# Another order of products and direct sub-tiles in the first column pairs of the retention output projection

## The chip, the cores and the metric

The kernel runs on one core of a Trainium2 chip. The metric is the device time of one launch in microseconds (us). A core has a matrix engine (TensorE, "PE" in the profile, with its weight loads as "PEld"), a vector engine (VectorE, "DVE"), a scalar engine (ScalarE, "ACT"), GpSimd ("POOL") and SyncE ("SP"), which here only starts DMA transfers. Each works through its own instruction list in order; they wait for one another by semaphores. Matrix products land in PSUM banks, of which each holds 128 x 512 fp32 numbers.

## The reference

A decoder trunk of two layers on one sequence of 256 tokens and width 2048: layer 0 is gated linear attention (GLA, four heads), layer 1 is retention (eight heads). Each layer widens to 4096, has a SiLU gate and a residual, and a last RMS norm follows.

```
h = x
h = h + gla_mixer(rms_norm(h, gla_norm[0]), ...)        # layer 0
h = h + retention_mixer(rms_norm(h, ret_norm[0]), ...)  # layer 1
return rms_norm(h, final_norm)

def retention_mixer(h, positions, w_in, gn_g, gn_b, w_out):
    q, k, v, gate = split(h @ w_in)         # widths 2048, 2048, 4096, 4096
    ... rotary q/k, chunked retention, group norm -> o   # 256 x 4096
    return (o * silu(gate)) @ w_out         # 4096 -> 2048
```

The change concerns only this last product, `@ w_out` of the retention layer: 256 tokens, 4096 inputs, 2048 outputs, all fp32.

## The kernel before, in words

**Weights and products.** All weights are streamed from HBM as sub-tiles of 256 input rows by 512 columns (512 KB), through eight raw buffers (`NRAW`, L29). SP starts the load of a raw buffer as soon as the buffer's last reader is done (`emit_raws`, L249; L243). For an fp32 product on PE each sub-tile is split in two parts: `hi`, a rounded copy by ACT (L287), and `lo`, the rest, a subtraction on DVE (L288), into pairs of split tiles of which there are four. Splits are made `LOOK` = 3 sub-tiles ahead of their use (`emit_split` L273, `next_weights` L315). The activations are split in the same way beforehand, and each product is made of three matmuls, hi x hi, hi x lo and lo x hi (`three`, L392 to L397). A sub-tile that is used for 128 tokens and two input slices, or one with all 256 tokens, comes to 6 or 12 matmuls of 512 columns.

**The output product in halves.** The 4096 inputs are the eight heads' outputs; the output product is done in two halves, after four heads each (`out_half`). The first half's output tiles are named `ra`, the second half's `rb`; each has four groups of 512 columns. Groups 0 and 1 are always done as a pair (`out_pair`, L959, tiles `rae` and `rbe`). `ra` has a second pair, groups 2 and 3; in `rb` group 2 (`rb2`, banks `rb_ps`) is a plain group and group 3 is the tail (`out_tail`, L1078), in matmuls of 256 columns (`tail_ps`), with the final norm behind it.

**A pair.** A pair takes two neighbouring groups, the one called v (group c) and the one called g (group c+1). The products of their first four sub-tiles are done by a Strassen-like scheme: seven block products instead of eight, on sums of weights and on sums of activations (`rsum`). The tokens P1, P2, P3, P5, P6, P7 and P8 are these products; each needs two split sub-tiles and 12 matmuls. The other four sub-tiles of each group are used directly for all 256 tokens: tokens v4 to v7 and g4 to g7, one split sub-tile and 12 matmuls each. The order of the tokens is a string: `UNIT` for most pairs, `LATE` for the first pair of each retention half (`out_order`, L147). The token `z` only marks where the two v sub-tiles for the sums are loaded.

**Sums of raw weights.** P1 uses x (the first two g sub-tiles), P3 uses z (v's third and fourth). Both are then changed in place in their raw buffers: accumulating DMAs that POOL starts (L296) add further sub-tiles from HBM to them, and two DVE adds (L282) make x += z ahead of P6. P5 uses x after the first two v sub-tiles were added to it, P7 uses z after `z += v` (v's first two), P8 uses x after `x += g` (g's third and fourth). In `_plan` (`pair`, L72) each sub-tile carries, in `post`, the accumulating DMAs that are to be started behind its split.

**Banks.** A pair has four banks, `B, A, C, V1`, and one of a pool of two (`lev`) for P5. P1, P6, P7 go through A one after the other, each taken out before the next begins; P8 stays in A and the g sub-tiles of the second 128 tokens are added to it there, up to g7. P2 begins B, in which the g sub-tiles of the first 128 tokens follow. P3 begins C; C and V1 take the v sub-tiles.

**Joins.** What a bank holds is joined to the residual `resid` in SBUF by one DVE instruction of 128 x 512: an add (L993) or a subtraction (L995). For P7, ACT copies the bank out first (`u3`, L1025). Joins are put off by one token in the program (`pend`).

**Who sets the order.** The token strings set the order of the program text. A planner then orders the instructions of each engine anew by its own estimate of times, under what depends on what, so that side work (the last head's norm and gating, transposes `rot_tp`, tiles `ro`, `ogt`) is laid between the tokens, and single matmuls of a neighbouring sub-tile can be drawn ahead. Each engine's list is fixed from then on.

Of the kernel before, what the change touches and what calls it, by code (L numbers as in the profile page):

```python
# [10 lines left out]
F32 = mybir.dt.float32  # L11
# [6 lines left out]
P = 128  # L18
# [4 lines left out]
GW = 512  # L23
SUB = 2
NSUB = NKT // SUB
# [30 lines left out]
def _plan():  # L56


    loads, subs = [], []

    def load(gid, j):
        loads.append((gid, j))
        return len(loads) - 1

    def use(c, pre=None, post=()):
        subs.append((c, pre, post))

    def plain(gid, js=range(NSUB)):
        for j in js:
            use(load(gid, j))  # L70

    def pair(g, v, q=None, order=None):  # L72
        order = (order or UNIT).split()
        x = [load(g, 0), load(g, 1)] if order[0] == "P1" else []
        z = []
        later = max(("P3", "P6"), key=order.index)
        for n, tok in enumerate(order):
            kind, i = tok[0], tok[1:]
            if kind in "qvg":
                plain({"q": q, "v": v, "g": g}[kind], [int(i)])  # L80
            elif tok == "z":
                z += [load(v, 2), load(v, 3)]
            elif tok == "P2":
                plain(g, [2, 3])
            else:
                if tok == "P1" and not x:
                    x += [load(g, 0), load(g, 1)]
                for j in range(2):
                    post = []
                    if tok == later:  # L90
                        post.append((z[j], (v, j)))
                    if tok == "P1":
                        post.append((x[j], (v, j)))
                    if tok == "P6":
                        post.append((x[j], (g, 2 + j)))
                    use(z[j] if tok in ("P3", "P7") else x[j], z[j] if tok == "P6" else None, post)

    def out_cols_of(name, half, joint):
        for c in (0, 2):
            cols = [(name, half, c + n) for n in range(2)]  # L100
            if joint[c // 2]:
                pair(cols[1], cols[0], order=out_order(name, c))
                continue
            for x in cols:
                plain(x)

    for half in range(2):
        for h in (2 * half, 2 * half + 1):
            plain(("aqk", h))
            for g in (2 * h, 2 * h + 1):  # L110
                if g in JOINT["a"]:
                    pair(("ag", g), ("av", g))
                else:
                    plain(("av", g))
                    plain(("ag", g))
        out_cols_of("ao", half, JOINT["ao", half])
    for half in range(2):
        for h in range(4 * half, 4 * half + 4):
            pair(("rg", h), ("rv", h), ("rqk", h), ret_order(h))
# [12 lines left out]
    for c in range(len(loads)):  # L132
        b = min(range(NRAW), key=lambda n: free[n])
        buf.append(b)
        free[b] = last[c]
    return loads, subs, places, last, buf
# [4 lines left out]
WHOLE = " ".join(f"q{j}" for j in range(NSUB)) + " " + UNIT  # L141


LATE = "P1 v4 z P3 v5 P5 P6 P2 v6 P7 g4 g5 v7 P8 g6 g7"


def out_order(name, c):  # L147
    return LATE if (name, c) == ("ro", 0) else UNIT

# [16 lines left out]
def kernel(  # L166
# [33 lines left out]
    lev_p = pool("lev", 2, space=psum)  # L200
# [200 lines left out]
    def product(ps, left, stop=False):  # L401
        for j in range(2):
            hi, lo = next_weights()
            for q in range(SUB):
                k = j * SUB + q
                three(ps, left(k, 0), left(k, 1), hi, lo, q, stop and k == QK - 1)

    def direct(lhs, ps, j, stop=False):
        hi, lo = next_weights()
        for t in range(2):  # L410
            cols = slice(t * P, (t + 1) * P)
            for q in range(SUB):
                kt = j * SUB + q
                three(ps[t], lhs[:, kt, 0, cols], lhs[:, kt, 1, cols], hi, lo, q, stop and q == SUB - 1)
# [544 lines left out]
    def out_pair(c, first, final, name):  # L959
        lhs, s = ogt, cur["s"]  # L960
        B, A, C, V1 = acc(4, f"{name}e{c}_ps", which=list(slots))
        slots.rotate(-2)
        P5 = lev_p.tile([P, GW], F32, tag="lev", name=f"{name}e{c}_p5")
        plain = lambda kt0, t: lambda k, a: lhs[:, kt0 + k, a, t * P : (t + 1) * P]
        summed = lambda i: lambda k, a: s[i][:, k, a, :]
        u3 = t4_p.tile([P, 2, GW], F32, tag="t4", name=f"{name}e{c}_u3")[:, 0, :]

        if final:
            for col in (c, c + 1):
                norm_row(col)  # L970

        def whole(col, t):
            if not first:
                square_sum(t, col)
            if final:
                dst = cur["resid"][:, t, col * GW : (col + 1) * GW]
                nc.vector.tensor_tensor(dst, dst, fns[col], ALU.mult)

        onward = not (first or final)
        late = deque([out_transposes(c)] if onward else [])  # L980

        def turn():
            advance()
            if late:
                next(late[0], None)

        g = c + 1
        tt_done, pend = set(), []

        def join(col, t, src, op=ALU.add, mark=None):  # L990
            dst = cur["resid"][:, t, col * GW : (col + 1) * GW]
            if op == ALU.add:
                keep(nc.vector.tensor_tensor(dst, src, dst, ALU.add))  # L993
            else:
                keep(nc.vector.tensor_tensor(dst, dst, src, ALU.subtract))  # L995
            tt_done.add((col, t, mark))
            if all((col, t, m) in tt_done for m in parts[col - c][t]):
                whole(col, t)

        parts = ((("5", "6", "v"), ("5", "7", "v")), (("1", "g"), ("g",)))  # L1000
        products = {
            "P1": lambda: product(A, plain(0, 0), stop=True),
            "P2": lambda: product(B, plain(4, 0)),
            "P3": lambda: product(C, summed(0)),
            "P5": lambda: product(P5, summed(1), stop=True),
            "P6": lambda: product(A, summed(2), stop=True),
            "P7": lambda: product(A, summed(3), stop=True),
            "P8": lambda: product(A, plain(4, 1)),
        }
        joins = {  # L1010
            "P1": lambda: join(g, 0, A, mark="1"),
            "P5": lambda: [join(c, t, P5, mark="5") for t in range(2)],
            "P6": lambda: join(c, 0, A, ALU.subtract, "6"),
            "P7": lambda: join(c, 1, u3, ALU.subtract, "7"),
            "v7": lambda: [join(c, t, x, mark="v") for t, x in enumerate((C, V1))],
        }
        toks = [x for x in out_order(name[0] + "o", c).split() if x != "z"]
        for n, tok in enumerate(toks):
            if tok[0] == "P":
                products[tok]()  # L1020
            else:
                direct(lhs, (C, V1) if tok[0] == "v" else (B, A), int(tok[1:]), stop=tok[1:] == str(NSUB - 1))
            if tok == "P7":
                with tc.high_priority():
                    keep(nc.scalar.activation(u3, A, AF.Copy))  # L1025
            while pend:
                pend.pop(0)()
            if tok in joins:
                pend.append(joins[tok])
            if n < 4:  # L1030
                advance()
                step()
                if n == 3:
                    drain_side()
            elif tok in ("g5", "P8", "g6"):
                turn()
        join(g, 0, B, mark="g")
        join(g, 1, A, mark="g")
        if onward:
            for _ in late[0]:  # L1040
                pass
            tasks.append(out_transposes(g))
        begun.clear()
        closed.clear()
# [212 lines left out]
    def ret_head(h):  # L1257
# [276 lines left out]
```

## Time and profile before

| what | us |
|---|---|
| median of three runs | 1383.75 (1382.77 to 1383.86) |
| the profiled execution's own time | 1382.14 |
| its span in the profile | 1380.3 |
| PE busy | 1363.0 (99%) |
| DVE busy | 1105.1 (80%) |
| ACT busy | 850.0 (62%) |
| POOL busy | 142.2 (10%) |
| weight loads started by SP | 447, median 5.0 to landing |
| accumulating and other weight DMAs started by POOL | 96, median 7.2 to landing |

Times inside the profile count from the start of the span. The first pair of the first half (`rae`) lies at about 924 to 968 us, that of the second half (`rbe`) at about 1280 to 1327, the plain group and the tail at 1327 to 1380. A row of a timeline gives start, duration, engine, line, operation, output and inputs, and in brackets how long the engine had stood idle before it and who released it. A row of waits gives engine, what waited, whom it waited for, the sum in us, how often, and the longest. A PE row's duration is that of one matmul, of which the next begins before it ends; the time between two starts is what counts.

### The profile page before, as it was taken

The numbers are of one execution on the slowest core, as the hardware profiler recorded it, in microseconds if no ns is written. First come the engines' busy times: TensorE is split into PE (matmuls) and PEld (weight loads), VectorE is DVE, ScalarE is ACT, GpSimd is POOL, SyncE is SP. The second block draws the span as 40 slices with busy tenths as digits, with TensorE's granted clock in tenths as the row PEclk, the third lists the DMA queues.
The fourth block names the chain that finished last, engine by engine and source line by source line (L and its number), as shares of the span: only waits on it lengthen the run. The fifth ranks groups of instructions, "written<-read, shape, count | busy, mean of one in ns | idle before, by whom it ended". The sixth has DMA issues, their size and how long they took to land.

```text
span 1380.3 us, 18486 instructions
## 1 busy us (share of the span) xinstructions
PE 1363.0 (99%) x6608; PEld 1142.2 (83%) x6608; DVE 1105.1 (80%) x1533; ACT 850.0 (62%) x1122; POOL 142.2 (10%) x200
## 2 busy tenths in 40 slices
PE   9999999999999999999999999999999999999997
PEld 7888888888888888888888888887888888888787
DVE  6686795987778887769888898988868897888883
ACT  6576656655567747566666665665546666666562
POOL 1003020110021021001011010101100101011100
PEclk9999999999999999999999999999999999999999
DMA  9755555789658657868898887898898787889771
GB/s 365 249 175 166 175 168 183 170 243 346 195 157 266 193 177 197 305 168 248 283 304 204 253 206 242 212 305 248 214 365 233 218 276 190 248 215 314 186 269 62
DMA packets 85085, 317.15 MB, mean 230 GB/s; under 512 B 9840, under 2 KB 10864, under 8 KB 83712
## 3 DMA queue, kind: packets, MB, share of 16 engines
q1 hardware_dynamic: 66768, 240.55, 49.5%
q0 software_dynamic: 16784, 68.03, 24.9%
q10 hardware_dynamic: 1440, 7.38, 1.4%
q8 instruction: 52, 0.85, 0.2%
q14 instruction: 41, 0.34, 0.1%
HBM read 305.44 MB, written 10.49 MB: 229 GB/s over the span
## 4 chain that ended last, share of the span: by engine, by line
PE 93%; DVE 3%; DMA 2%; issue 1%; ACT 1%; POOL 0%; DVEq 0%; SPq 0%; ACTq 0%
PE rqk_ps L368 8%; PE re_ps L395 8%; PE re_ps L396 8%; PE re_ps L397 8%; PE rqk_ps L369 4%; PE gqk_ps L368 4%; PE gg_ps L326 3%; PE gv_ps L325 3%; PE gv_ps L326 3%; PE gv_ps L327 3%; PE gg_ps L327 3%; PE gg_ps L325 3%; DMA raw<-in_w_all 2%; PE ge_ps L396 2%; PE ge_ps L397 2%; PE ge_ps L395 2%
## 5 line engine op out<-in xcount | busy, mean ns | idle before, releaser
L288 DVE TENSOR_TENSOR lo<-raw,hi 128x1024 fp32r<-128x1024 f32 (+1 forms) x569 | 687.2, 1220 | 199.9 <-ACT hi L287 193.4
L287 ACT ACTIVATE hi<-raw 128x1024 fp32r<-128x1024 f32 (+1 forms) x569 | 596.1, 1056 | 385.3 <-DMA raw<-in_w_all 57.3
L368 PE MATMUL rqk_ps<-xhl,hi 128*128 128x512 f32 x480 | 161.7, 396 | 0.0
L296 POOL DMA_DIRECT2D raw<-in_w_all x96 | 83.0, 869 | 542.7 <-DVE lo L288 257.7
L396 PE MATMUL re_ps<-lo,xhl 128*128 128x512 f32 x352 | 137.3, 390 | 0.0
L397 PE MATMUL re_ps<-hi,xhl 128*128 128x512 f32 x352 | 137.1, 390 | 0.0
L395 PE MATMUL re_ps<-hi,xhl 128*128 128x512 f32 x352 | 131.7, 391 | 0.0
L369 PE MATMUL rqk_ps<-xhl,lo 128*128 128x256 f32 x480 | 121.4, 281 | 0.0
L368 PEld LDWEIGHTS rqk_ps<-xhl,hi 128*128 128x128 f32 x480 | 89.3, 188 | 17.5
L369 PEld LDWEIGHTS rqk_ps<-xhl,lo 128*128 128x128 f32 x480 | 87.5, 189 | 3.7
L397 PEld LDWEIGHTS re_ps<-hi,xhl 128*128 128x128 f32 x352 | 66.1, 188 | 13.7
L396 PEld LDWEIGHTS re_ps<-lo,xhl 128*128 128x128 f32 x352 | 66.1, 188 | 13.2
L395 PEld LDWEIGHTS re_ps<-hi,xhl 128*128 128x128 f32 x352 | 66.0, 188 | 13.3
L368 PE MATMUL gqk_ps<-xhl,hi 128*128 128x512 f32 x216 | 76.5, 398 | 0.0
L326 PE MATMUL gg_ps<-lo,xhl 128*128 128x512 f32 x192 | 75.4, 393 | 0.0
L326 PE MATMUL gv_ps<-lo,xhl 128*128 128x512 f32 x192 | 75.2, 392 | 0.0
L325 PE MATMUL gv_ps<-hi,xhl 128*128 128x512 f32 x192 | 75.1, 393 | 0.0
L327 PE MATMUL gv_ps<-hi,xhl 128*128 128x512 f32 x192 | 75.0, 391 | 0.0
L327 PE MATMUL gg_ps<-hi,xhl 128*128 128x512 f32 x192 | 74.9, 390 | 0.0
L325 PE MATMUL gg_ps<-hi,xhl 128*128 128x512 f32 x192 | 74.8, 391 | 0.0
L810 POOL TENSOR_TENSOR s<-s,m 128x64 f32<-128x64 f32 x56 | 36.1, 676 | 233.2 <-DVE m L801 223.9
L369 PE MATMUL gqk_ps<-xhl,lo 128*128 128x256 f32 x216 | 59.0, 280 | 0.0
(422 smaller groups left out, 2686.1 us busy)
## 6 DMA issues: line engine op xcount, KB each, us to landing
raw<-in_w_all SPq DMA_DIRECT2D x447, 512.0 KB, 5.0
raw<-in_w_all POOLq DMA_DIRECT2D x96, 512.0 KB, 7.2
resid<-in_x_n SPq DMA_DIRECT2D x2, 1024.0 KB, 8.6
gg<-in_gn_g POOLq DMA_DIRECT2D x8, 256.0 KB, 4.0
resid_x<-resid ACTq DMA_DIRECT2D x1, 2048.0 KB, 9.0
gb<-in_gn_b POOLq DMA_DIRECT2D x8, 256.0 KB, 7.4
gb_resid<-resid_x POOLq DMA_DIRECT2D x1, 2048.0 KB, 11.9
resid_g<-gb_resid ACTq DMA_DIRECT2D x1, 2048.0 KB, 9.9
```

The lines of the kernel that those rows point to most:

```text
L287: a = nc.scalar.activation(hi[:, sl], src[:, sl], AF.Copy)
L288: b = nc.vector.tensor_tensor(lo[:, sl], src[:, sl], hi[:, sl].bitcast(F32), ALU.subtract)
L296: nc.gpsimd.dma_start(raws[n], block(key), accum_op=ALU.add)
L325: mm(ps, xh, hi[:, q, :], start=kt == 0, stop=False)
L326: mm(ps, xh, lo[:, q, :], start=False, stop=False)
L327: mm(ps, xl, hi[:, q, :], start=False, stop=kt == NKT - 1)
L368: mm(ps[c], wh, rhs[:, kt, :, :], start=kt == 0, stop=False)
L369: mm(ps[c][:, 0, :], wl, rhs[:, kt, 0, :], start=False, stop=False)
L395: mm(ps, xh, hi[:, q, :], start=start, stop=False, **again)
L396: mm(ps, xh, lo[:, q, :], start=False, stop=False, **again)
L397: mm(ps, xl, hi[:, q, :], start=False, stop=stop, **again)
L810: nc.gpsimd.tensor_tensor(dst, dst, side_of(m[:, li, :], z), ALU.add)
```

## The change

Three things change, all for the first pair (columns 0 and 1) of each retention half.

The string `LATE` becomes another order. Before: `P1 v4 z P3 v5 P5 P6 P2 v6 P7 g4 g5 v7 P8 g6 g7`. After: `P1 v4 z P3 g4 P5 v5 P6 P2 g5 P7 v6 P8 g6 v7 g7`: direct sub-tiles and products take turns, g4 and g5 come before P7, and v7 is last but one.

Since g4 now comes before P6 and P7 need bank A, the g sub-tiles of the second 128 tokens get a bank of their own, `G1`, the second one of the pool `lev`. P8 then ends in bank A and is joined on its own (mark `8`), and the join of `G1` follows g7: one more join per pair.

In the plan, the accumulating DMAs `x += g` are no longer started behind P6's own two sub-tiles' splits in the `post` list of those, but are kept in `owed` and go with the next direct sub-tile or with P2's first: those of `z += v` come first. This part of the code holds for all pairs.

```
--- before.py
+++ after.py
@@ -74,14 +74,18 @@
         x = [load(g, 0), load(g, 1)] if order[0] == "P1" else []
         z = []
         later = max(("P3", "P6"), key=order.index)
+        owed = []
         for n, tok in enumerate(order):
             kind, i = tok[0], tok[1:]
             if kind in "qvg":
-                plain({"q": q, "v": v, "g": g}[kind], [int(i)])
+                use(load({"q": q, "v": v, "g": g}[kind], int(i)), post=owed)
+                owed = []
             elif tok == "z":
                 z += [load(v, 2), load(v, 3)]
             elif tok == "P2":
-                plain(g, [2, 3])
+                use(load(g, 2), post=owed)
+                plain(g, [3])
+                owed = []
             else:
                 if tok == "P1" and not x:
                     x += [load(g, 0), load(g, 1)]
@@ -92,7 +96,7 @@
                     if tok == "P1":
                         post.append((x[j], (v, j)))
                     if tok == "P6":
-                        post.append((x[j], (g, 2 + j)))
+                        owed.append((x[j], (g, 2 + j)))
                     use(z[j] if tok in ("P3", "P7") else x[j], z[j] if tok == "P6" else None, post)
 
     def out_cols_of(name, half, joint):
@@ -141,7 +145,7 @@
 WHOLE = " ".join(f"q{j}" for j in range(NSUB)) + " " + UNIT
 
 
-LATE = "P1 v4 z P3 v5 P5 P6 P2 v6 P7 g4 g5 v7 P8 g6 g7"
+LATE = "P1 v4 z P3 g4 P5 v5 P6 P2 g5 P7 v6 P8 g6 v7 g7"
 
 
 def out_order(name, c):
@@ -961,6 +965,10 @@
         B, A, C, V1 = acc(4, f"{name}e{c}_ps", which=list(slots))
         slots.rotate(-2)
         P5 = lev_p.tile([P, GW], F32, tag="lev", name=f"{name}e{c}_p5")
+        order = out_order(name[0] + "o", c)
+        G1 = A
+        if order == LATE:
+            G1 = lev_p.tile([P, GW], F32, tag="lev", name=f"{name}e{c}_g1")
         plain = lambda kt0, t: lambda k, a: lhs[:, kt0 + k, a, t * P : (t + 1) * P]
         summed = lambda i: lambda k, a: s[i][:, k, a, :]
         u3 = t4_p.tile([P, 2, GW], F32, tag="t4", name=f"{name}e{c}_u3")[:, 0, :]
@@ -997,7 +1005,7 @@
             if all((col, t, m) in tt_done for m in parts[col - c][t]):
                 whole(col, t)
 
-        parts = ((("5", "6", "v"), ("5", "7", "v")), (("1", "g"), ("g",)))
+        parts = ((("5", "6", "v"), ("5", "7", "v")), (("1", "g"), ("g", "8") if G1 is not A else ("g",)))
         products = {
             "P1": lambda: product(A, plain(0, 0), stop=True),
             "P2": lambda: product(B, plain(4, 0)),
@@ -1005,7 +1013,7 @@
             "P5": lambda: product(P5, summed(1), stop=True),
             "P6": lambda: product(A, summed(2), stop=True),
             "P7": lambda: product(A, summed(3), stop=True),
-            "P8": lambda: product(A, plain(4, 1)),
+            "P8": lambda: product(A, plain(4, 1), stop=G1 is not A),
         }
         joins = {
             "P1": lambda: join(g, 0, A, mark="1"),
@@ -1014,12 +1022,14 @@
             "P7": lambda: join(c, 1, u3, ALU.subtract, "7"),
             "v7": lambda: [join(c, t, x, mark="v") for t, x in enumerate((C, V1))],
         }
-        toks = [x for x in out_order(name[0] + "o", c).split() if x != "z"]
+        if G1 is not A:
+            joins["P8"] = lambda: join(g, 1, A, mark="8")
+        toks = [x for x in order.split() if x != "z"]
         for n, tok in enumerate(toks):
             if tok[0] == "P":
                 products[tok]()
             else:
-                direct(lhs, (C, V1) if tok[0] == "v" else (B, A), int(tok[1:]), stop=tok[1:] == str(NSUB - 1))
+                direct(lhs, (C, V1) if tok[0] == "v" else (B, G1), int(tok[1:]), stop=tok[1:] == str(NSUB - 1))
             if tok == "P7":
                 with tc.high_priority():
                     keep(nc.scalar.activation(u3, A, AF.Copy))
@@ -1035,7 +1045,7 @@
             elif tok in ("g5", "P8", "g6"):
                 turn()
         join(g, 0, B, mark="g")
-        join(g, 1, A, mark="g")
+        join(g, 1, G1, mark="g")
         if onward:
             for _ in late[0]:
                 pass
```

More of the change, by code (lines that the diff above doesn't have):

```diff
@@ L76, in pair @@
         later = max(("P3", "P6"), key=order.index)
+        owed = []
         for n, tok in enumerate(order):
@@ L79, in pair @@
             if kind in "qvg":
-                plain({"q": q, "v": v, "g": g}[kind], [int(i)])
+                use(load({"q": q, "v": v, "g": g}[kind], int(i)), post=owed)
+                owed = []
             elif tok == "z":
@@ L83, in pair @@
             elif tok == "P2":
-                plain(g, [2, 3])
+                use(load(g, 2), post=owed)
+                plain(g, [3])
+                owed = []
             else:
@@ L94, in pair @@
                     if tok == "P6":
-                        post.append((x[j], (g, 2 + j)))
+                        owed.append((x[j], (g, 2 + j)))
                     use(z[j] if tok in ("P3", "P7") else x[j], z[j] if tok == "P6" else None, post)
@@ L141 @@
 WHOLE = " ".join(f"q{j}" for j in range(NSUB)) + " " + UNIT
-LATE = "P1 v4 z P3 v5 P5 P6 P2 v6 P7 g4 g5 v7 P8 g6 g7"
+LATE = "P1 v4 z P3 g4 P5 v5 P6 P2 g5 P7 v6 P8 g6 v7 g7"
 def out_order(name, c):
@@ L963, in out_pair @@
         P5 = lev_p.tile([P, GW], F32, tag="lev", name=f"{name}e{c}_p5")
+        order = out_order(name[0] + "o", c)
+        G1 = A
+        if order == LATE:
+            G1 = lev_p.tile([P, GW], F32, tag="lev", name=f"{name}e{c}_g1")
         plain = lambda kt0, t: lambda k, a: lhs[:, kt0 + k, a, t * P : (t + 1) * P]
@@ L998, in join @@
                 whole(col, t)
-        parts = ((("5", "6", "v"), ("5", "7", "v")), (("1", "g"), ("g",)))
+        parts = ((("5", "6", "v"), ("5", "7", "v")), (("1", "g"), ("g", "8") if G1 is not A else ("g",)))
         products = {
@@ L1007, in out_pair @@
             "P7": lambda: product(A, summed(3), stop=True),
-            "P8": lambda: product(A, plain(4, 1)),
+            "P8": lambda: product(A, plain(4, 1), stop=G1 is not A),
         }
@@ L1016, in out_pair @@
         }
-        toks = [x for x in out_order(name[0] + "o", c).split() if x != "z"]
+        if G1 is not A:
+            joins["P8"] = lambda: join(g, 1, A, mark="8")
+        toks = [x for x in order.split() if x != "z"]
         for n, tok in enumerate(toks):
@@ L1021, in out_pair @@
             else:
-                direct(lhs, (C, V1) if tok[0] == "v" else (B, A), int(tok[1:]), stop=tok[1:] == str(NSUB - 1))
+                direct(lhs, (C, V1) if tok[0] == "v" else (B, G1), int(tok[1:]), stop=tok[1:] == str(NSUB - 1))
             if tok == "P7":
@@ L1037, in out_pair @@
         join(g, 0, B, mark="g")
-        join(g, 1, A, mark="g")
+        join(g, 1, G1, mark="g")
         if onward:
```

## The prediction

> **What bounds the kernel now.** I read the page first (busy shares, the chain that ended last), then PE's waits over the whole run, then the busy time of each engine in the stretches that the change touches, then single instructions.
>
> ```profile
> span 1380.3 us, 18486 instructions
> PE 1363.0 (99%) x6608; PEld 1142.2 (83%) x6608; DVE 1105.1 (80%) x1533; ACT 850.0 (62%) x1122; POOL 142.2 (10%) x200
> PE 93%; DVE 3%; DMA 2%; issue 1%; ACT 1%; POOL 0%; DVEq 0%; SPq 0%; ACTq 0%
> ```
>
> PE is busy 99% of the span and holds 93% of the chain. The change removes no matmul, so it can win only PE's waits, and adds time only by making new ones. All of PE's longest waits are these (us in total, times, longest):
>
> ```profile
> PE warm_ps L514 <- POOL warm L512: 1.8, 1, 1.8
> PE gqk_ps L356 <- ACT hi L287: 1.3, 1, 1.3
> PE rae_ps L395 <- DVE resid L995: 1.3, 1, 1.3
> PE rbe_ps L395 <- DVE resid L995: 1.3, 1, 1.3
> PE rbe_ps L395 <- ACT hi L287: 1.2, 1, 1.2
> PE rae_ps L395 <- ACT hi L287: 1.2, 1, 1.2
> ```
>
> Four of the six lie in the two pairs that the change rewrites (`rae`, `rbe`): 1.2 at P6 on the weight split, 1.3 at the first matmul of P7, which waits until L995 has taken P6 out of bank A. The next view (us; busy time of PE, PEld, DVE, ACT and POOL; PE clock; DMA share; GB/s) takes both pairs from P3 to that wait, and what follows:
>
> ```profile
> 929.50:951.90 22.40, 19.68 (x86) 14.85 (x84) 22.40 (x30) 11.86 (x13) 4.03 (x5) 1.00 0.65 148
> 951.90:966.30 14.40, 14.36 (x63) 11.91 (x64) 10.00 (x9) 8.23 (x9) 0.00 (x0) 1.00 1.00 377
> 1285.30:1307.70 22.40, 19.68 (x86) 14.83 (x84) 22.40 (x30) 11.85 (x13) 4.05 (x5) 1.00 0.64 146
> 1307.80:1327.10 19.30, 19.18 (x84) 15.55 (x85) 14.48 (x15) 10.71 (x13) 0.00 (x0) 1.00 0.98 356
> ```
>
> Here the whole-run average misleads: from P3 to the L995 join DVE is busy 22.40 of 22.40 us, PE only 19.68. In this stretch DVE is the bound; it is so because the split of each sub-tile (`lo`, one DVE instruction), the raw sums and the head's last side work meet. A product (P token) asks two splits for 12 matmuls, a direct sub-tile (v or g token) one split for 12. So what counts is how many matmuls PE has issued when DVE reaches the join that frees bank A.
>
> **The change part by part.** First the order.
>
> ```profile
> 951.95 0.50 PE L395 MATMUL rae_ps<-hi,rsum 128*128 128x512 f32 x1 [1.26 <-DVE resid L995]
> 952.28 0.40 PE L396 MATMUL rae_ps<-lo,rsum 128*128 128x512 f32 x1
> 949.61 0.39 PE L395 MATMUL rae_ps<-hi,ogt 128*128 128x512 f32 x1
> 950.07 0.39 PE L397 MATMUL rae_ps<-hi,ogt 128*128 128x512 f32 x1
> 948.95 2.35 DVE L288 TENSOR_TENSOR lo<-raw,hi 128x1024 fp32r<-128x1024 f32 x2
> 951.22 0.67 DVE L995 TENSOR_TENSOR resid<-resid,rae_ps 128x512 f32<-128x512 f32 x1
> ```
>
> A 512-wide matmul follows the one before by 0.23 us (950.07 − 949.61 for two); I take 0.2267, the step over longer runs without a wait (a sub-tile of 12 is 2.72). Before, eight tokens stand ahead of P7 (P1 v4 P3 v5 P5 P6 P2 v6), and one matmul of the next direct sub-tile is pulled in: 97 matmuls by 951.95. After, nine stand ahead (P1 v4 P3 g4 P5 v5 P6 P2 g5) and two matmuls of v6: 110. So 13 matmuls, 13 × 0.2267 = 2.95 us, move under DVE's cover. For that DVE has one more split ahead of the join: two splits end to start take 951.22 − 948.95 = 2.27, so one is 1.14. Gain 2.95 − 1.14 = 1.81 per pair. Splits of the new order are late at two points (P2's second sub-tile, then g5), so PE waits there, some 0.5 and 1.0 us, instead of at P6 and P7; these lie inside the 1.81, and only a further restart costs: a step over a wait is 952.28 − 951.95 = 0.33 instead of 0.23, so 0.1. Net 1.7 per pair.
>
> The own bank G1 and the further join: without it P8 and the g half would share bank A up to g7; now P8 leaves A by a join of its own, one DVE add more per pair.
>
> ```profile
> L993 DVE TENSOR_TENSOR resid<-rae_ps,resid x10: 677/682/690, 931.9 to 1012.1; 128x512 f32<-128x512 f32 x10
> ```
>
> 0.68 us of DVE, after P8, where DVE is busy 10.00 of 14.40 (row 951.90:966.30): 4.4 us are free, I cost it at 0; without that cover it would be 0.68 per pair. G1 is the second bank of a pool whose last readers are long done; 0. `stop` on P8 is a flag; 0.
>
> `owed` puts the accumulating DMAs of x += g behind those of z += v. The order of POOL's queue and of SP's is the same in both programs, instruction for instruction, so it costs nothing in issue; what moves is time, and what the transfers meet.
>
> ```profile
> 937.40 2.35 DVE L282 TENSOR_TENSOR raw<-raw,raw 128x1024 f32<-128x1024 f32 x2
> 939.15 0.90 POOL L296 DMA_DIRECT2D raw<-in_w_all  x1 [0.82 <-DVE raw L282]
> 940.29 0.87 POOL L296 DMA_DIRECT2D raw<-in_w_all  x1 [0.23 <-issue]
> DMA to landing us min/median/max: 6.1/6.7/7.2
> 947.61 2.01 ACT L287 ACTIVATE hi<-raw 128x1024 fp32r<-128x1024 f32 x2 [1.17 <-DMA raw<-in_w_all]
> 940.88 4.62 DVE L288 TENSOR_TENSOR lo<-raw,hi 128x1024 fp32r<-128x1024 f32 x4
> 944.39 1.46 SPq L243 DMA_DIRECT2D raw<-in_w_all  x2
> 953.24 1.06 ACT L287 ACTIVATE hi<-raw 128x1024 fp32r<-128x1024 f32 x1 [3.62 <-DMA raw<-in_w_all]
> DMA to landing us min/median/max: 3.7/7.2/11.5
> 1311.72 0.39 PE L395 MATMUL rbe_ps<-hi,ogt 128*128 128x512 f32 x1
> 1312.22 0.50 PE L396 MATMUL rbe_ps<-lo,ogt 128*128 128x512 f32 x1
> ```
>
> The z += v pair (939.15, 940.29; landing 6.1 to 7.2) feeds P7's splits. Before, the later one lands at 947.6, when ACT starts (947.61); its `hi` is done at 948.7, DVE takes it at 950.1: 1.4 us to spare. After, g4's split stands ahead of the raw sums of 937.40, so sums, transfers and DVE's need of them all come 1.14 later and the 1.4 stays. The x += g pair is needed by P8, after P7 and v6, 12 to 13 us after its issue, against a slowest landing of 11.5 in 922 to 972. I take 0 for both.
>
> The weight load that SP issues at 944.39 waits for a buffer that the third of the four splits from 940.88 frees. In the new order g4's split frees it: begun at 937.40, done 1.2 later, 938.6, so 5.7 us earlier. ACT's 3.62 us on that load goes; in the first pair this wait costs PE nothing, in the second PE loses 1312.22 − 1311.72 − 0.23 and the second step of a restart there, 0.44 over its whole passage from P7 to g7: a gain of 0.44. But this load now runs beside the z += v pair. Its 0.5 MB at the 377 GB/s of the row 951.90:966.30 take 1.4 us of the DMA engines, just what is to spare: 0. At 146 GB/s (row 1285.30:1307.70) it is 3.6 and P7 would be 2.2 late: that end belongs to rival C.
>
> What is late next: v7 now stands last but one, so banks C and V1 are joined late. In the first pair the column group behind it takes them: one wait of about 0.15 at its start, against the gain. First pair: 1.7 − 0.15 ≈ 1.55. In the second, the planned order of PE puts six 256-wide matmuls of the very last column (`tail_ps`) between g7 and column 2, so as not to wait for those banks, then one that wants the tail's second sub-tile. But the tail's first weights then have no 24 matmuls of column 2 ahead of them.
>
> ```profile
> 1327.05 1.06 ACT L287 ACTIVATE xhl<-raw 128x1024 fp32r<-128x1024 f32 x1 [1.37 <-DMA raw<-in_w_all]
> 1327.09 0.39 PE L325 MATMUL rb_ps<-hi,ogt 128*128 128x512 f32 x1
> 1371.66 0.28 PE L326 MATMUL tail_ps<-tail,ogt 128*128 128x256 f32 x1
> 1371.78 0.28 PE L327 MATMUL tail_ps<-xhl,ogt 128*128 128x256 f32 x1
> DMA to landing us min/median/max: 4.0/4.8/4.9
> DMA to landing us min/median/max: 4.2/4.4/4.6
> DMA to landing us min/median/max: 4.9/5.5/8.1
> ```
>
> Call g7's end T (before: 1327.09). The first tail load leaves when column 2's first split is done; that split waits for a pair of split tiles, four deep. Before, P8's first half frees them, after, its second half, which ends at T − 3 × 2.72 = T − 8.16; with ACT 1.06, DVE 1.22 and the hand-overs, 2.59 in all, the load leaves at T − 5.57. With a landing L, then ACT's 1.06 and DVE's 1.22, PE waits L − 3.28 (hand-overs included). The six matmuls take 6 × 0.12 (1371.78 − 1371.66), the second load left one sub-tile (2.72) later: a second wait of 0.85, then 0.15 for v7's join. Together L − 2.28, for L of 3.3 or more. The landings of raw loads issued in 1316 to 1322, 1322 to 1328 and 1308 to 1316 are the last three rows in that order. The new issue time is about 1320, near the first and second; I take L = 4.4: 2.1 us. Ends of the range: no wait at all, and L = 8.1, 5.8 us.
>
> The Trainium skill (DMA: Bandwidth & Descriptors, "Anatomy of one DMA — SWDGE (gpsimd) path") gives a transfer about 2.0 us fixed and its bytes at 436 GB/s; an estimate from it for 512 KB is 3.2 us, by which the end wait would be 0.9 and the time 1381.0. The page states it for GpSimd's path, and the traced 4.0 to 4.9 of these SyncE loads, beside others in flight (DMA share 0.98), lies above it; so the rows decide.
>
> Second pair: 1.7 + 0.44 − 2.1 ≈ 0.05. Sum: 1.55 + 0.05 = 1.6 us. The profiled execution took 1382.14 (span 1380.3 and 1.84 around it), 1.61 below the median 1383.75. A span of 1378.7 gives 1380.5 profiled and **1382.1** on the median's basis.
>
> **The rivals.** *A, faster: the end wait is not met.* If the tail's loads land in 3.2 us or less, or leave earlier than I place them, 0.9 us of waits or nothing remain. With nothing the gain is 1.55 + 1.7 + 0.44 ≈ 3.7: 1380.1. For it: 3.7 is seen elsewhere (the row of 922 to 972). Against: no landing there is under 4.0.
>
> *B, slower: the tail's loads land late.* Each us of L costs one us; the sum is zero at L = 6.0 and 2.77 us (0.2%) slower from L = 8.8. For it: 11.5 is seen beside the accumulating transfers of the first pair. Against: those issued after 1316 took 4.9 at most. With L = 9 the wait is 6.7 and the time 1386.8; with 8.1 it is 1385.9.
>
> By the Trainium skill (TensorE: Matmul & The Clock Gate, "Part 1: The HAM clock gate") PE's clock drops to half after an idle window of about 3.4 us. PE's two waits so far, 2.5 us in 22, left the granted clock at 1.00, so no row shows it here; it would make B worse only.
>
> *C, the change does not do what it says: P7's wait stays.* If the earlier load delays the z += v pair beyond the 1.4 us, P7's splits are late, and with them the join behind them on DVE. Late by 1.8, the order's gain is gone in that pair. In both pairs that takes 3.4 off the sum of 1.6: 1385.6; in one, 1383.9. For it: these rows have the DMA engines' share at 0.64 with the accumulating transfers alone, and they are slow (146 GB/s). Against: the load leaves 1.6 us ahead of them, while the engines have little to do.
>
> **How the numbers follow.** Forecast 0.43, A 0.25, B 0.15, C 0.17. A measurement of this kernel tells 0.2% (2.77 us) from no change. A gain above that (below 1381.0) is A alone: 0.25. The forecast and C (to 1.9 above the time before) are within: 0.60. B is slower: 0.15. The likeliest case's own range, L from 3.3 to 5.2, is 1381.1 to 1383.0. The range for 8 in 10 runs from 1379.9, just below A's full gain, to 1385.6, the end of C, which leaves out the outer part of B.
>
> **What would show it.** In the profile after: PE's 1.2 on ACT `hi` gone in both pairs, 1.3 on L995 down to some 0.15, and in their place waits of some 0.5 and 1.0 on DVE `lo` ahead of P7; DVE still full from P3 to the L995 join, 1.1 us longer; the load of 944.39 leaving near 938.6; ACT's 3.62 gone; at the end of the second pair `tail_ps` waiting about 1.1 on DVE and 0.85 on ACT. Wrong would be: a wait of 1 us or more at P7 with ACT waiting for a raw DMA ahead of it (C), no `tail_ps` wait (A), or one above 4 (B), or DVE joins late enough to hold up column 2 of either half by more than 0.5.

## The result and the profile after

The changed kernel takes 1388.7 us (median of 6 runs, 1387.19 to 1390.46) against 1383.78; the ratio is 1.0037, 95% interval 1.0024 to 1.005. Measured a second time later it took 1388.09 (ratio 1.0027, 1.0018 to 1.0036). It is slower by 4 to 5 us, where 1.6 us less were forecast, and lies above the range (1379.9 to 1385.6). The profiled execution took 1387.19 with a span of 1385.4.

First PE's waits in the changed kernel (its lines are numbered four to ten higher than before: L291 is ACT's `hi`, L292 DVE's `lo`, L399 to L401 the three matmuls, L1003 the subtracting join, L1035 ACT's copy of P7's bank, `rae_u`).

```profile
PE warm_ps L518 <- POOL warm L516: 1.8, 1, 1.8
PE tail_ps L329 <- ACT xhl L291: 1.7, 1, 1.7
PE gqk_ps L360 <- ACT hi L291: 1.5, 1, 1.5
PE rae_ps L399 <- ACT rae_u L1035: 1.0, 1, 1.0
PE tail_ps L330 <- DVE tail L292: 0.9, 1, 0.9
PE rae_ps L400 <- DVE lo L292: 0.9, 2, 0.7
PE rbe_ps L400 <- DVE lo L292: 0.9, 2, 0.7
PE rbe_ps L399 <- ACT rbe_u L1035: 0.8, 1, 0.8
```

The four waits of before (1.2 on `hi`, 1.3 on L995, in each pair) are gone, as forecast, and the two on DVE's `lo` stand in their place, as forecast. New, or larger than forecast, are the waits of P8 for `rae_u` and `rbe_u` and those of the tail at the end of the second pair.

Where the time went can be read from four starts: the first matmul of each pair, the end of the second pair (g7's end), and the last matmul of all. The lines of the tiles give first and last start.

```profile
L399 PE MATMUL rae_ps<-hi,ogt x80: 388/389/499, 925.8 to 1012.0; 128*128 128x512 f32 x80
...
L401 PE MATMUL rbe_g<-hi,ogt x8: 388/389/393, 1291.6 to 1327.0; 128*128 128x512 f32 x8
...
L331 PE MATMUL tail_ps<-xhl,ogt x64: 278/283/415, 1330.5 to 1376.9; 128*128 128x256 f32 x64
```

And of the kernel before:

```profile
L395 PE MATMUL rae_ps<-hi,ogt x88: 388/389/503, 924.9 to 1011.2; 128*128 128x512 f32 x88
...
L327 PE MATMUL tail_ps<-xhl,ogt x64: 279/283/283, 1338.7 to 1371.8; 128*128 128x256 f32 x64
```

| stretch, us | before | changed | difference |
|---|---|---|---|
| start to the first pair's first matmul (the same program in both) | 924.9 | 925.8 | +0.9 |
| both pairs of the first half (`rae_ps`, first to last row above) | 86.3 | 86.2 | −0.1 |
| second pair: first matmul (1280.6; 1281.4) to g7's end (1327.1; 1327.2) | 46.5 | 45.8 | −0.7 |
| g7's end to the last tail matmul | 44.7 | 49.7 | +5.0 |

The first row is most likely chance: in twelve profiles of kernels that are the same up to there, the first pair began between 924.9 and 927.6, and the one profile of before is the earliest of them. The run with everything but the order (below) takes as long as the kernel before, and its first pair began at 926.7. The loss is the last row: 5.0 us between g7 and the end. The third row is worth less than it looks: with the old order the second pair took 46.5 here and 45.8 in the run with everything but the order, so one profile does not tell 0.7 from nothing.

PE at that place, in the changed kernel:

```profile
1326.99 0.39 PE L401 MATMUL rbe_g<-hi,ogt 128*128 128x512 f32 x1
1329.03 0.38 PE L329 MATMUL tail_ps<-xhl,ogt 128*128 128x256 f32 x1 [1.66 <-ACT xhl L291]
1330.29 0.41 PE L330 MATMUL tail_ps<-tail,ogt 128*128 128x256 f32 x1 [0.88 <-DVE tail L292]
...
1331.35 0.42 PE L329 MATMUL tail_ps<-xhl,ogt 128*128 128x256 f32 x1
1332.03 0.79 PE L329 MATMUL rb_ps<-hi,ogt 128*128 128x512 f32 x1 [0.27 <-DVE resid L1001]
1332.62 0.63 PE L330 MATMUL rb_ps<-lo,ogt 128*128 128x512 f32 x1
1333.05 0.63 PE L331 MATMUL rb_ps<-hi,ogt 128*128 128x512 f32 x1
...
1334.16 0.39 PE L331 MATMUL rb_ps<-hi,ogt 128*128 128x512 f32 x1
```

Column 2 (`rb_ps`) begins at 1332.03, 4.81 us after g7's end (1326.99 + 0.23 = 1327.22); seven tail matmuls at 0.12 account for 0.84 of that, so 3.97 are lost ahead of it. Then column 2's first matmuls follow each other by 0.43 instead of 0.23: five steps take 2.13 (1334.16 − 1332.03) instead of 1.13, another 1.0. The windows show why; columns as in the forecast, the clock is the third number from the end.

```profile
1327.20:1329.00 1.80, 0.17 (x1) 0.00 (x0) 0.00 (x0) 1.08 (x2) 0.00 (x0) 1.00 0.58 237
...
1330.30:1331.30 1.00, 1.00 (x5) 1.00 (x6) 1.00 (x2) 1.00 (x2) 0.00 (x0) 0.61 0.00 0
1331.30:1332.30 1.00, 0.73 (x4) 0.44 (x3) 1.00 (x3) 0.81 (x2) 0.00 (x0) 0.50 0.00 0
...
1334.20:1336.00 1.80, 1.80 (x10) 1.47 (x9) 1.24 (x3) 0.88 (x1) 0.00 (x0) 1.00 0.42 102
```

The granted clock falls to 0.50 some 3 us after g7's end and is back at 1.00 by 1334.2. Part of the slow stretch lies in the tail matmuls ahead of column 2.

ACT and DVE there, and at P8 of the first pair (timeline of the changed kernel):

```profile
1327.92 1.06 ACT L291 ACTIVATE xhl<-raw 128x1024 fp32r<-128x1024 f32 x1 [4.89 <-DMA raw<-in_w_all]
...
1329.01 1.23 DVE L292 TENSOR_TENSOR tail<-raw,xhl 128x1024 fp32r<-128x1024 f32 x1 [4.72 <-ACT xhl L291]
1330.15 1.22 DVE L292 TENSOR_TENSOR lo<-raw,hi 128x1024 fp32r<-128x1024 f32 x1
1331.29 0.68 DVE L1001 TENSOR_TENSOR resid<-rbe_ps,resid 128x512 f32<-128x512 f32 x1
...
954.93 1.06 ACT L291 ACTIVATE hi<-raw 128x1024 fp32r<-128x1024 f32 x1 [1.78 <-DMA raw<-in_w_all]
958.81 1.06 ACT L291 ACTIVATE hi<-raw 128x1024 fp32r<-128x1024 f32 x1 [2.82 <-DMA raw<-in_w_all]
959.77 0.58 ACT L1035 ACTIVATE rae_u<-rae_ps 128x512 f32<-128x512 f32 x1
...
960.40 0.50 PE L399 MATMUL rae_ps<-hi,ogt 128*128 128x512 f32 x1 [0.96 <-ACT rae_u L1035]
```

Both places read alike. At the end, the join that frees column 2's bank (1331.29) stands in DVE's list behind the tail's first split, which waits 4.72 us for ACT, which waits for the tail's first load. v7's own matmuls ended where g7's began, 2.72 ahead of g7's end, at about 1324.5, so the join stood some 7 us in the list with its data ready. At P8, the copy that frees bank A (959.77) stands in ACT's list behind P8's two splits, and the second of these waits 2.82 us for its accumulated transfer.

### The profile page after: what moved, and what is told of

Its sections match the earlier page's. It is cut to its first block, busy times and chain, and to the rows that moved or that the text cites. A ratio compares the mean times of both kernels' runs of the same rounds, so it can differ in the third digit from the quotient of the medians.

```text
span 1385.4 us, 18486 instructions
## 1 busy us (share of the span) xinstructions
PE 1366.2 (99%) x6608; PEld 1143.6 (83%) x6608; DVE 1106.3 (80%) x1535; ACT 850.2 (61%) x1122; POOL 142.2 (10%) x200
## 4 chain that ended last, share of the span: by engine, by line
PE 91%; DMA 3%; DVE 2%; issue 2%; ACT 1%; POOL 0%; DVEq 0%; SPq 0%; ACTq 0%; POOLq 0%
PE rqk_ps L372 8%; PE re_ps L399 8%; PE re_ps L401 8%; PE re_ps L400 8%; PE rqk_ps L373 4%; PE gqk_ps L372 4%; DMA raw<-in_w_all 3%; PE gg_ps L330 3%; PE gv_ps L331 3%; PE gv_ps L330 3%; PE gv_ps L329 3%; PE gg_ps L329 3%; PE gg_ps L331 3%; PE ge_ps L401 2%; PE ge_ps L399 2%; PE ge_ps L400 2%
## 5 line engine op out<-in xcount | busy, mean ns | idle before, releaser
L292 DVE TENSOR_TENSOR lo<-raw,hi 128x1024 fp32r<-128x1024 f32 (+1 forms) x569 | 687.9, 1221 | 201.3 <-ACT hi L291 195.2
L291 ACT ACTIVATE hi<-raw 128x1024 fp32r<-128x1024 f32 (+1 forms) x569 | 596.5, 1057 | 390.7 <-DMA raw<-in_w_all 58.1
L401 PE MATMUL re_ps<-hi,xhl 128*128 128x512 f32 x352 | 137.2, 390 | 0.0
L399 PE MATMUL re_ps<-hi,xhl 128*128 128x512 f32 x352 | 131.8, 391 | 0.0
L401 PEld LDWEIGHTS re_ps<-hi,xhl 128*128 128x128 f32 x352 | 66.1, 188 | 13.8
L399 PEld LDWEIGHTS re_ps<-hi,xhl 128*128 128x128 f32 x352 | 66.0, 188 | 13.2
L400 PEld LDWEIGHTS re_ps<-lo,xhl 128*128 128x128 f32 x352 | 66.1, 188 | 13.1
```

The costliest lines, as they stand in the source:

```text
L291: a = nc.scalar.activation(hi[:, sl], src[:, sl], AF.Copy)
L292: b = nc.vector.tensor_tensor(lo[:, sl], src[:, sl], hi[:, sl].bitcast(F32), ALU.subtract)
L399: mm(ps, xh, hi[:, q, :], start=start, stop=False, **again)
L400: mm(ps, xh, lo[:, q, :], start=False, stop=False, **again)
L401: mm(ps, xl, hi[:, q, :], start=False, stop=stop, **again)
```

## The experiments

Each is the changed kernel with the edit shown; where nothing else is said, the token order was edited alone. All were timed beside runs of the kernel before on the same chip (medians 1383.6 to 1383.8).

**The clock at the end.**

```diff
+        if name == "rb" and c == 0:
+            fill = lev_p.tile([P, GW], F32, tag="lev", name="fill")
+            for _ in range(8):
+                keep(mm(fill, lhs[:, 0, 0, 0:P], lhs[:, 0, :, :], start=True, stop=True))
         join(g, 0, B, mark="g")
```

> The changed kernel with eight matmuls more (128x512, read by nobody) between g7 of the second half's first pair and the tail's first matmul, where PE stood 1.81 us in the changed kernel's profile. Clock theory: the granted clock fell to 0.50 because PE did almost nothing from g7's end to 3 us later; with the stand filled the clock stays at 1.00 and the time falls by what the slow steps cost, about 1.5 us (0.5 in the six tail matmuls, 1.0 in the first five of column 2): 1387.2. The waits on the tail's load stay. Rival, that the clock fell for another reason or that the slow steps cost nothing in the end: no gain, 1388.7.

Measured: 1387.48 (ratio 1.0032, 1.0019 to 1.0044). By time alone that is not told apart from the changed kernel. The profile tells it: with the eight matmuls in PE's stand, the clock stays at 1.00 (window 1332 to 1336 of this run):

```profile
1332.00:1333.00 1.00, 0.47 (x3) 0.19 (x1) 0.94 (x1) 1.00 (x3) 0.00 (x0) 1.00 0.00 0
...
1335.00:1336.00 1.00, 0.92 (x4) 0.80 (x5) 1.00 (x2) 0.72 (x2) 0.00 (x0) 1.00 0.63 78
```

And the timeline of PE in it:

```profile
1335.08 0.50 PE L329 MATMUL rb_ps<-hi,ogt 128*128 128x512 f32 x1 [0.72 <-DVE resid L1001]
```

From g7's end (1330.35) to the last tail matmul (1379.1) it is 48.8 instead of 49.7. So between these two profiles the clock accounts for 0.9, the slow first steps of column 2. The slow tail matmuls cost nothing: column 2 begins 4.73 after g7's end (4.81 in the changed kernel), since it waits for DVE's join (0.72 here) whether PE is quick or not. The other 4 us of the end are waits.

**v7 earlier, in two steps.**

```diff
-LATE = "P1 v4 z P3 g4 P5 v5 P6 P2 g5 P7 v6 P8 g6 v7 g7"
+LATE = "P1 v4 z P3 g4 P5 v5 P6 P2 g5 P7 v6 P8 v7 g6 g7"
```

> The changed kernel with v7 one token earlier (P8 v7 g6 g7), so banks C and V1 are joined before g7 ends and PE begins with column 2. End theory: the wait on the tail's first load and the clock drop behind it are gone, 4.9 us: about 1383.8; the wait at P8 for the copy of P7's bank (0.96 and 0.85) stays. Rival, that the loss lies in the pairs themselves: 1388 or little less.

Measured: 1382.75 (ratio 0.9995, 0.9987 to 1.0004). The end is 44.7 again, no `tail_ps` wait is left, and the waits for the copy of P7's bank stay, beside one of 0.8 on a split:

```profile
PE rbe_ps L399 <- ACT rbe_u L1035: 1.0, 1, 1.0
...
PE rbe_ps L399 <- ACT hi L291: 0.8, 1, 0.8
...
PE rae_ps L399 <- ACT rae_u L1035: 0.4, 1, 0.4
```

One token moved by one place takes back the whole loss. A loss in the pairs themselves, the rival, is not there.

```diff
-LATE = "P1 v4 z P3 g4 P5 v5 P6 P2 g5 P7 v6 P8 g6 v7 g7"
+LATE = "P1 v4 z P3 g4 P5 v5 P6 P2 g5 P7 v6 v7 P8 g6 g7"
```

> The changed kernel with v7 two tokens earlier (P7 v6 v7 P8 g6 g7). End theory: as in the run with v7 before g6, 4.9 us. Queue theory: ACT's copy of P7's bank stands behind only one of P8's two splits, whose raw data land at 954.9 in the first pair, and two direct sub-tiles lie between P7 and P8, so the wait at P8 is gone as well: 1.0 and 0.85 less, in sum about 1382.0; if also the order's gain comes out whole, 1380.4. Rival, that DVE remains the bound and the wait only moves: as with v7 before g6, 1383.8.

Measured: 1380.76 (ratio 0.9978, 0.9969 to 0.9987): faster than the kernel before, near the 1380.4 of the case in which the order's gain comes out whole. No wait on `rae_u` or `rbe_u` is left. PE's waits in the second pair:

```profile
PE rbe_ps L400 <- DVE lo L292: 0.9, 2, 0.7
PE rot_tp L692 <- DVE ro L1183: 0.2, 1, 0.2
```

The stretches are 84.5 (first half's pairs; 86.3 before), 44.2 (second pair; 46.5) and 44.7 (end): gains of 1.8 and 2.3, against 1.7 and 2.14 in the forecast's terms for the order and the load. (Against the 45.8 of the second pair in the run with everything but the order the 2.3 would be 1.6.) So the forecast's mechanism for the order was right; in the changed kernel P8's wait and the end hid it. This edit takes one split from ahead of the copy and puts one sub-tile more between P7 and P8; which of the two removes P8's wait, the run does not tell.

**One half alone.** `out_order` is told the half; the other half has the old order and bank A.

```diff
...
+PAST = "P1 v4 z P3 v5 P5 P6 P2 v6 P7 g4 g5 v7 P8 g6 g7"
-def out_order(name, c):
-    return LATE if (name, c) == ("ro", 0) else UNIT
+def out_order(name, c, half):
+    if (name, c) != ("ro", 0):
+        return UNIT
+    return LATE if half == 0 else PAST
...
```

> The new order, own bank and further join in the first half's pair only; the second half's pair has the old order and bank A. End theory: the second half is as before, and the first pair's gain (13 matmuls under DVE's cover) is eaten by the wait at P8: 1383.7, no difference to before. Rival, that both pairs lose alike: half of 4.9, 1386.2. Rival, that the loss is spread over the run (0.9 us lay ahead of the first pair in the one profile): 1384.6.

Measured: 1384.54 (ratio 1.0006, 0.9996 to 1.0015): no difference from before, and less than half of the loss. The interval (1383.1 to 1385.7 us) holds both the 1383.7 of the theory and the 1384.6 of the second rival, a loss spread over the run; the run of the other half, next, speaks against that rival.

With `half == 1` in the last line:

> The new order, own bank and further join in the second half's pair only; the first half's pair as before. End theory: the second pair itself is 0.7 faster (gain of the order less the 0.85 at P8), the end behind it 5.0 slower: 4.3 in sum, 1388.0, that is nearly the whole loss. Rival, that both pairs lose alike: 1386.2. With the first-half run at 1384.5, a sum of the two that differs from the whole change by over 1.5 would say that they are not independent.

Measured: 1389.35 (ratio 1.0038, 1.0026 to 1.005), a little over the 1388.0 of the theory and far from 1386.2: the second half holds the whole loss. Its end takes 49.8, the end of the first-half run 44.7. The losses of the two runs, 0.9 and 5.7, add up to 1.7 more than the whole change's 4.9, over the 1.5 named beforehand; with intervals of 1.3 to 1.7 us to either side of each this is no sign of a dependence.

**Everything but the order.**

```diff
-LATE = "P1 v4 z P3 g4 P5 v5 P6 P2 g5 P7 v6 P8 g6 v7 g7"
+LATE = "P1 v4 z P3 v5 P5 P6 P2 v6 P7 g4 g5 v7 P8 g6 g7"
```

> The old order with everything else of the change: own bank G1, stop on P8, one join more per pair, owed. If these cost nothing, as forecast: 1383.8. If the further join lies on the path: 0.68 per pair, 1385.1.

Measured: 1383.31 (ratio 0.9998, 0.999 to 1.0007). Own bank, further join and `stop` cost nothing, as forecast. `owed` does nothing here: without it the changed kernel's instructions are the same on every engine.

The profile of this run shows one thing more. The pairs have the old order and its wait at P6 (1.2), and behind that wait the granted clock fell to 0.50 in both pairs, from 943.7 and from 1298.7 on, for 3.4 us each time. The first pair's windows:

```profile
940.30:943.70 3.40, 1.94 (x10) 1.03 (x9) 3.40 (x5) 3.01 (x4) 1.78 (x2) 1.00 0.62 107
943.80:947.10 3.30, 3.29 (x8) 2.65 (x9) 3.30 (x4) 2.20 (x4) 1.71 (x2) 0.50 1.03 202
```

The pairs took no longer for it: 86.4 (first half, 86.3 before) and 45.8 (46.5 before). DVE is busy throughout both windows, and the time that PE lost in slow matmuls went off its wait on L995, which was 1.3 before and is not listed here. So the slow clock cost time only where PE was the bound, as behind g7.

**Further orders**, all with the own bank. First g5 between P6 and P2 and v6 ahead of P7 (the order with ten tokens ahead):

```diff
-LATE = "P1 v4 z P3 g4 P5 v5 P6 P2 g5 P7 v6 P8 g6 v7 g7"
+LATE = "P1 v4 z P3 g4 P5 v5 P6 g5 P2 v6 P7 v7 P8 g6 g7"
```

> A further order with the own bank: P1 v4 z P3 g4 P5 v5 P6 g5 P2 v6 P7 v7 P8 g6 g7. Ten tokens stand ahead of P7 and none of P6, P2 and P7 follows another product, one direct sub-tile lies between P7 and P8. DVE theory: the waits on DVE's lo (0.2 and 0.7 per pair, with a restart each) go as well, about 1.2 per pair less than with v7 before P8 (1380.8): 1378.4. The queue theory says that with only v7 between P7 and P8 the copy of P7's bank is again behind both splits of P8; but all of it comes later against the transfers, P7 being one token later, so a wait of 0 to 0.3. Rival, that loads become the bound, 9 to 10 us to landing in this stretch and needed one token sooner: 1381 to 1383, with waits on ACT hi that waits for a raw DMA.

Measured: 1381.45 (ratio 0.9984, 0.9975 to 0.9993). The rival held: the waits on `lo` are gone, and loads are the bound, by one wait of 2 us in each pair, behind ACT's waits for raw data. In the first pair of this profile the clock fell to 0.50 behind that wait as well, from 959.7 on, for eight steps of 0.43 instead of 0.23: 1.6 us more, which the second pair does not have. The first pair's waits:

```profile
ACT hi L291 <- DMA raw<-in_w_all: 6.3, 3, 2.6
...
PE rae_ps L399 <- ACT hi L291: 2.0, 1, 2.0
```

Then v6 ahead of P7 alone (`P2 g5 v6 P7 v7 P8 g6 g7` at the end of the string):

> P1 v4 z P3 g4 P5 v5 P6 P2 g5 v6 P7 v7 P8 g6 g7: as with v7 before P8, but v6 moved ahead of P7. DVE theory: v6's 12 matmuls follow g5 with one split for them, so the 0.2 wait ahead of g5 and one restart go, 0.3 to 0.6 per pair: 1379.5 to 1380.2. Load theory (as in the order with ten tokens ahead): v7's load, late beside the accumulating transfers, is needed one token sooner against them, and PE waits up to 2 us on ACT's hi: 1381.5.

Measured: 1378.84 (ratio 0.9961, 0.9948 to 0.9973), the fastest here: 5.0 below the kernel before (0.7 below the lower end of the DVE theory). In the pairs no wait on a load is left, one of 0.7 on `lo` per pair is. This order, too, has ten tokens ahead of P7, so these alone do not make the loads the bound; why v7's load holds PE up in the one order and not in the other, the runs do not show. In both, only one sub-tile lies between P7 and P8, and neither profile lists a wait on the copy of P7's bank. That P7 comes later against the transfers would explain it, and is not shown by itself.

And g5 between P6 and P2 alone (`P6 g5 P2 P7 v6 v7 P8 g6 g7`):

> P1 v4 z P3 g4 P5 v5 P6 g5 P2 P7 v6 v7 P8 g6 g7: as with v7 before P8, but g5 moved between P6 and P2. The same nine tokens stand ahead of P7, so the loads and the join of P7 keep their places. DVE theory: the splits are spread more evenly, PE's waits on lo fall from 0.9 to some 0.4 per pair, 0.5 to 0.9 less per pair: 1379.0 to 1379.8. Rival, that P2 and P7 in sequence, four splits for 24 matmuls, let P7 wait for its splits as much as is won: 1380.8.

Measured: 1379.96 (ratio 0.997, 0.9958 to 0.9981), just above the DVE theory's 1379.0 to 1379.8. In its profile PE's waits on `lo` are gone altogether, and stretches are 83.8, 43.5 and 44.7. Whether this order or the one before it is faster, the runs don't tell: their intervals overlap.

**The changed kernel again**, beside the last two:

> The changed kernel itself once more, beside the two orders of this call. 1388.7 as before; its profile shows whether the clock drop at the end of the second pair (0.50 in the one profile so far) comes every time: the end theory expects the stand of PE between g7 and column 2 at 3 to 4 us again, in g7's end to the last tail matmul 49.7 (44.7 in the kernel before).

Measured: 1388.09. The end took 49.8, with waits of 1.0, 0.9 and 0.7, and the clock at 0.50 again, now from about 1331.4 on, for column 2's first seven steps:

```profile
1328.39 0.39 PE L329 MATMUL tail_ps<-xhl,ogt 128*128 128x256 f32 x1 [1.04 <-ACT xhl L291]
1329.65 0.38 PE L330 MATMUL tail_ps<-tail,ogt 128*128 128x256 f32 x1 [0.87 <-DVE tail L292]
...
1331.38 0.80 PE L329 MATMUL rb_ps<-hi,ogt 128*128 128x512 f32 x1 [0.71 <-DVE resid L1001]
...
1334.89 0.39 PE L331 MATMUL rb_ps<-hi,ogt 128*128 128x512 f32 x1
```

The sum is that of the first profile, its parts are not. Column 2 begins 4.19 after g7's end (1327.19), so 3.35 are lost ahead of it, not 3.97; its first eight steps take 3.51 instead of 1.81, so the clock costs 1.7, not 1.0. That both ends come to 5.0 is in part chance. The wait at P8 was 0.3 in the first pair and not listed in the second: it varies from one execution to the next.

## Why the prediction was wrong, step by step

**What bounds the kernel before, and the order's gain: right.** DVE is the bound from P3 to P7 in the changed kernel too (22.68 of 22.70 us below), and 13 matmuls moved under its cover (110 of the pair's matmuls are issued ahead of P7, 97 before).

```profile
931.40:954.10 22.70, 21.62 (x94) 16.40 (x93) 22.68 (x29) 12.20 (x13) 4.04 (x5) 1.00 0.68 158
```

P7's wait fell to 0.17 (second pair; it is not listed in the first), the waits on `lo` came where they were placed (0.2 and 0.7 for 0.5 and 1.0), and where nothing else stood against it, with v7 before P8, the pairs gained 1.8 and 2.3 us.

**The load that leaves earlier: right.** It left at 939.6 in a profile that runs 0.9 late there: 938.7, for 938.6. The z += v pair, beside it, took 7.4 and 8.7 us to landing instead of 6.1 and 7.2, so 1.3 and 1.5 more, which the 1.4 us to spare about took up. Rival C came this near.

**Own bank, further join, `owed` in issue: right**, 0 by the run with everything but the order. That `owed` puts the z += v transfers first is no change: they were first before.

**The x += g pair, "I take 0": wrong, the first failed step.** The forecast asked when PE needs P8's splits (12 to 13 us after the issue, against a slowest landing of 11.5). It did not ask what stands behind these splits in ACT's list. ACT's copy of P7's bank does, and P8 cannot begin in bank A before it. And with one direct sub-tile between P7 and P8 where three were, that copy is needed 2.72 us after P7's end and not 8.16. Landings of this pair were 10.4 and 13.1, later than the 8.6 and 11.5 of before:

```profile
L300 POOL DMA_DIRECT2D raw<-in_w_all x2: 851/854/858, 944.4 to 945.6; - x2
DMA to landing us min/median/max: 10.4/11.8/13.1
```

The waits were 0.96 and 0.85 in one profile, 0.3 and less in the other. Counted from one start to the next, with the slower step behind them, they come to 1.23 and 1.12, and to 0.6 and 0.4. With v7 before P8 they are gone, and the time is 2.0 us lower than with v7 before g6 (the intervals of these two runs meet at 0.9987). The first half's gain of 1.55 shrank to 0.1 in the first profile, of which 1.23 is P8 and 0.2 has no place; in the second it shrank to 0.2 with only 0.6 at P8. So this step explains the first half's loss in the one profile, and in the other only in part.

**The end, "L − 2.28 with L = 4.4": the right mechanism, mis-sized, and one piece missing.** The tail's matmuls were pulled ahead and waited for the tail's first load; the forecast's rival B has this place. The load landed 5.5 us after its issue, not 4.4, and left at 1322.4, 4.8 before g7's end and not 5.57 (the split ahead of it was the last of three in DVE's list, from 1318.87 on).

```profile
raw<-in_w_all SPq DMA_DIRECT2D x1, 512.0 KB, 5.5
```

By the forecast's own formula that is 5.5 + 0.77 − 2.28 = 4.0, and 3.97 was measured. The term was 2.1. In the second profile the same load, again issued 4.8 ahead of g7's end, took 4.9, and the formula gives 3.4, where 3.35 was measured. Part of this fit is luck. The formula's last 1.0 is a wait of 0.85 for the tail's second load and 0.15 for v7's join. Neither profile has a wait on the second load; PE waited for the join instead, 0.27 and 0.71, behind the splits of the tail and of column 2 in DVE's list. The forecast named that among the signs of being wrong (joins that hold up column 2 by more than 0.5) and gave it only 0.15.

The missing piece is the clock, 1.0 in the first profile and 1.7 in the second: the forecast took it up only as something that would make rival B worse, for one wait longer than 3.4 us, since its one profile of before showed 1.00 beside waits of 1.2 and 1.3. In the changed kernel the stands ahead of the fall were 1.66 and 0.88, with matmuls between, and it came. With the old order it can come as well, as the run with everything but the order shows.

By the Trainium skill (TensorE: Matmul & The Clock Gate, "Part 1: The HAM clock gate") what halves the clock is an idle window of about 3.4 us, free-running. The two profiles agree in the half rate and in the length of the slow stretch, 3.4 us, but PE was not wholly idle in the 3.4 us ahead of it: two tail matmuls in the first, seven in the second.

**Sum.** 0.1 + 0.7 − 5.0 is 4.2 us of loss, as against a gain of 1.6. With 0.9 ahead of the first pair that makes the 5.1 by which the two profiled spans differ. In the second profile the pairs gain 0.2 and 1.8 and the end loses 5.1: a loss of 3.1, with the rest of the difference in stretches where the program is the same. So the pairs' shares are known to about 1 us, the end's to about 0.1. That the profile of before was an early one (1.61 below its median) was seen in the forecast, and set right by taking the median as the basis.

## What to carry to other kernels

When a step is moved nearer to its predecessor, look in each engine's list for what stands ahead of the instruction that frees the bank between them: a copy or a join behind a split that waits for a transfer inherits that wait, and it counts from the time at which the copy is needed, not the split. An order can be right in what it hides and lose everything at its end; v7 two tokens earlier in the string turned +5 us into −3. Where an engine is the bound in a stretch only, spread its work between the steps that ask most of it, until the next thing (here the loads, in one of the further orders) takes over.

## What the runs showed of the hardware

The granted clock of PE can fall to 0.50 after two short waits (1.0 and 0.9 us) with small matmuls between them, and came back 3.4 us later each time; eight matmuls that nobody reads, laid into the stand, kept it at 1.00, and the end was 0.9 us shorter. It fell after single waits of 1.2 us with transposes behind them (everything but the order, both pairs; in the kernel before, the same wait left it at 1.00) and of 2.0 us (ten tokens ahead, first pair). The runs show no length of wait above which it falls. What it cost ranged from nothing, where DVE was the bound, to 1.7 us. Four accumulating transfers of 512 KB started within 4.4 us of each other took 7.4, 8.7, 10.4 and 13.1 us to landing; a plain load started 1.6 us ahead of them took 4.5, and the next four plain loads behind them 8.8 to 10.1.
